# Diagonal of a 2-D prefix sum: row sums split by rows instead of columns, and the last 16 rows loaded early

## The chip, the cores and the metric

The kernel runs on one core of a Trainium2 chip. The metric is the device time of one execution in microseconds (us). Three runs of the kernel before took 667.54, 667.44 and 667.08 us; the median is 667.44.

## What is computed

```python
def setup_inputs():
    B, H, W = 4, 4224, 4224
    return {"x": np.random.randn(B, H, W).astype(np.float32)}

def reference(x):
    B, H, W = x.shape
    ps = np.cumsum(np.cumsum(x, axis=1), axis=2)
    N = min(H, W)
    diag = np.diagonal(ps, axis1=1, axis2=2)
    return np.cumsum(diag, axis=1).astype(np.float32)
```

Element i of an image's diagonal is the sum of the square x[0..i, 0..i]. It grows from i-1 to i by the part of row i left of and on the diagonal and the part of column i above it. So the kernel needs, for each i, one row sum up to the diagonal and one column sum down to it, and then two running sums over i. Every element of the four images is read once: 285 MB in float32.

## The kernel before, in words

**Staging.** An image has 11 groups of 384 rows and columns (GW = 384, NG = 11). The main loop takes strips of 768 rows: a strip is a tile `strip` of 128 partitions x 6 rows x 4224 columns in bf16, loaded by one DMA from GpSimd (POOL) that casts from float32 on the way (`load_rows`, L76). Images 0 to 2 take five such strips and one of 384 rows; the last image (LB = 3) takes four strips, two half strips, and then a finely cut end. There are three strip buffers (NBUF = 3), so the load of a strip waits until the strip three places earlier has been used up; POOL stands at that wait in program order. Nothing plans the order: instructions run on each engine as the program lists them.

**One strip** (`add_up`, L349). TensorE (PE) adds the columns right of the diagonal block with matmuls by a one-hot matrix (L226, L219). VectorE (DVE) multiplies the diagonal block by a mask (`mu`, L362) and subtracts (L363), so that the block keeps only the part left of the diagonal; where the next group's columns are summed by rows (`rowed`, L268), DVE does it next. Row sums then go up to column `hi`, the end of the diagonal block. They are split **by columns**: ScalarE (ACT) sums columns 0 to `ws` of each of the six rows (`act_sum`, L263, writing its unneeded copy to a tile `dump`), with ws = 9/16 of the block's first column, and DVE sums columns `ws` to `hi` of all six rows in one instruction (`acc`, L268). The two halves are added later (`sum_up`, L387).

**The end of the last image.** Its last 256 + 128 rows come in pieces: rows of `part_a` in two DMAs (L451), and the last 128 rows in five (L462). These five split 32 rows at a time into four pieces of 1024 columns each, so that 32 rows fill 128 partitions: blocks 0, 1, 2 whole, block 3 as columns 0 to 768 and 768 to 1024 of each quarter. POOL can have eight of these DMAs under way; the last two L462 issues wait for earlier landings. DVE (`pair_sum`, L277) and ACT (L263) add up what landed, PE weighs the sums into three small PSUM rows (`fin_a`, `fin_b`, `fin_e`, L219), and SyncE (SP) stores the results (L558 to L581). The very last chain is: landing of the last piece, `pair_sum`, three matmuls into `fin_e`, a copy (L580) and a store (L581).

**Other traffic.** `head`, the last 528 columns of 256 rows, is loaded first by SP's queue without a cast (L69) and used up at the start. Four images' results leave by SP: 11 rows of 3 x 384 at L558 (about 525 us), 10 rows of 384 at L561, and three single rows.

Of the kernel before, what the change touches and what calls it, by code (L numbers as in the profile page):

```python
# [17 lines left out]
def kernel(  # L18
# [30 lines left out]
    consts = ctx.enter_context(tc.tile_pool(name="consts", bufs=1))  # L49
    strips = ctx.enter_context(tc.tile_pool(name="strips", bufs=NBUF))  # L50
    mup = ctx.enter_context(tc.tile_pool(name="mup", bufs=1))
    dumpool = ctx.enter_context(tc.tile_pool(name="dump", bufs=1))
    smalls = ctx.enter_context(tc.tile_pool(name="smalls", bufs=2))
    last = ctx.enter_context(tc.tile_pool(name="last", bufs=1))
    psum_d = ctx.enter_context(
# [156 lines left out]
    weights4 = consts.tile([P, P], FP32, name="weights4")  # L212
    nc.vector.tensor_scalar_max(out=weights4, in0=steps, scalar1=0.0)

    ident_h = consts.tile([P, P], BF16, name="ident_h")
    nc.vector.tensor_copy(out=ident_h, in_=ident)

    def matmul(o, lhsT, rhs, start=False):
        nc.tensor.matmul(  # L219
            o, lhsT=lhsT, rhs=rhs, start=start, stop=False, skip_group_check=True  # L220
        )
# [36 lines left out]
    def act_sum(acc, src, own=None):  # L258
        w = src.shape[-1]
        dump = own  # L260
        if dump is None:
            dump = dumpool.tile([P, 2176], BF16, name="dump")
        nc.scalar.activation(  # L263
            out=dump[:, :w], in_=src, func=ACT.Copy, accum_out=acc
        )

    def row_sums(acc, src):
        nc.vector.reduce_sum(out=acc, in_=src, axis=AX.X)  # L268
# [26 lines left out]
            accum_out=acc,  # L295
        )

    def scalar_cols(r0):

        return r0 * 9 // 16 // 32 * 32  # L300
# [15 lines left out]
    for h in range(2):  # L316
        w = GW - h * P
        masked(hmu[:, h, :w], head[:, h, HC - w : HC], um1[:, :w], hu[:, h : h + 1])
    nc.vector.tensor_sub(out=asum[:, :, 0], in0=hs[:, 0:2], in1=hu[:, 0:2])

    whole_sums = last.tile([NG, LB, GW], FP32, name="whole_sums")
    last_sums = last.tile([NG, GW], FP32, name="last_sums")

    for b in range(B):
# [10 lines left out]
        def row_of(j):  # L335
            return (j + t0) % NG
# [9 lines left out]
            matmul(d[:, lo:hi], lhsT, rhs, start=first[0])  # L346
            first[0] = False

        def add_up(strip, f, r0, acc, um, wp=0, ws=None, by_rows=False):  # L349
# [8 lines left out]
            if ws is None:  # L358
                ws = scalar_cols(r0)
            mu = mup.tile([P, f, f * P], BF16, name=f"mu{f}")  # L360
            block = strip[:, :, r0:hi]
            nc.vector.tensor_mul(out=mu, in0=block, in1=um)  # L362
            nc.vector.tensor_sub(out=block, in0=block, in1=mu)  # L363
            if by_rows:
                rowed = mup.tile([P, GW], FP32, name="rowed")
                row_sums(
                    rowed,
                    strip[:, :, hi : hi + GW].rearrange("p q c -> p c q"),
                )
            for h in range(nw):  # L370
                for q in range(f):
                    columns(g + h, 0, GW, mu[:, q, h * GW : (h + 1) * GW], q > 0)
            if by_rows:
                k = row_of(g + nw)
                matmul(d, sel_f[:, NG - 1 - k : 2 * NG - 1 - k], rowed)
            for q in range(f):
                if ws > wp:
                    act_sum(acc[:, q, 0:1], strip[:, q, wp:ws])
            row_sums(acc[:, :, 1], strip[:, :, ws:hi])

        acc6 = smalls.tile([P, NS, F2, 2], FP32, name="acc6")
        acc3 = smalls.tile([P, 2, F, 2], FP32, name="acc3")
        nc.vector.memset(acc6[:, 0, :, 0], 0.0)

        def sum_up(acc):

            nc.vector.tensor_add(  # L387
                out=acc[..., 1], in0=acc[..., 1], in1=acc[..., 0]
            )

        ns = NS if whole else NS - 1
        for s in range(ns):
            strip = prefetched.pop(0) if prefetched else None
            if strip is None:
                strip = strip_tile()
                load_rows(strip, b, s * F2 * P)
            add_up(
                strip, F2, s * F2 * P, acc6[:, s], um6, by_rows=whole and s > 0
            )
            if not whole and s == 0:  # L400
                diag_b = last.tile([P, P], BF16, name="diag_b")
                nc.gpsimd.dma_start(out=diag_b, in_=x[b, TB:N, TB:N])
            if not whole and s == 1:
                row_sums(hs[:, 2:3], diag_b)
                masked(hmu[:, 2, :P], diag_b, um1[:, :P], hu[:, 2:3])
                nc.vector.tensor_sub(out=dtot, in0=hs[:, 2:3], in1=hu[:, 2:3])
                for h in range(3):
                    columns(LG, h * P, GW, hmu[:, h, : GW - h * P], h > 0)
        a6 = acc6[:, :ns]
        sum_up(a6)  # L410
        for h in range(2):
            ps = slice(h * HP, (h + 1) * HP)
            k = row_of(h)
            nc.vector.tensor_copy(  # L414
                out=r6[ps, k : k + 2 * ns : 2, :], in_=a6[ps, :, :, 1]
            )

        strip = strip_tile()
        if whole:
            load_rows(strip[:, :F], b, T0)  # L420
            add_up(strip[:, :F], F, T0, acc3[:, 0], um3)
            sum_up(acc3[:, 0])
            nc.vector.tensor_copy(out=r3[:, LG, :], in_=acc3[:, 0, :, 1])  # L423
        else:


            for h in range(2):
                load_rows(strip[:, h * F : h * F + F], b, T0 - (2 - h) * GW)
            add_up(strip[:, :F], F, T0 - 2 * GW, acc3[:, 0], um3)
            sum_up(acc3[:, 0])  # L430
            nc.vector.tensor_copy(out=r3[:, row_of(LG - 2), :], in_=acc3[:, 0, :, 1])
# [7 lines left out]
            add_up(strip[:, F:], F, T0 - GW, parts, um3, wp, ws)  # L439
            row_sums(parts[:, :, 2], fold_g)  # L440
            row_sums(r3[:, row_of(LG - 1), :], parts)

        if not whole:

            strip = strip_tile()
            part_a = strip[:, 0:2]
            part_b = strip[:, 2, :TB].rearrange("p (s c) -> p s c", s=4)
            spare = strip[:, 3, :]
            acuts = [(1536, N - HC), (0, 1536)]
            for c0, c1 in acuts:  # L450
                nc.gpsimd.dma_start(out=part_a[:, :, c0:c1], in_=src_a[:, :, c0:c1])  # L451
            CB = TB // 4
            bcut = 768
            for sb, c0, c1 in (
                (0, 0, CB),
                (1, 0, CB),
                (2, 0, CB),
                (3, 0, bcut),
                (3, bcut, CB),
            ):  # L460
                r0 = TB + sb * R
                nc.gpsimd.dma_start(  # L462
                    out=part_b[:, sb, c0:c1],
                    in_=x[b, r0 : r0 + R, :TB].rearrange("r (k c) -> r k c", k=4)[
                        :, :, c0:c1
                    ],
                )
# [112 lines left out]
        nc.vector.tensor_copy(out=ye, in_=fin_e)  # L580
        nc.sync.dma_start(out=out[b, T0 + E0 : N].unsqueeze(0), in_=ye)  # L581

# [29 lines left out]
```

## Time and profile before

| what | value |
|---|---|
| median of three runs | 667.44 us (667.08 to 667.54) |
| span of the profiled execution, first to last instruction | 665.7 us |
| own time of the profiled execution | not given by the page; the median lies 1.74 us above its span |
| DVE / PE / ACT / POOL busy | 379.8 / 214.2 / 135.3 / 31.7 us |
| DMA from POOL (queue 0) | 7312 packets, 142.47 MB written, 99.9% of 16 engines' time |
| DMA from SP (queue 1) | 342 packets, 0.61 MB, 0.3% |
| HBM read | 285.47 MB, 429 GB/s over the span |

The core has 16 DMA engines, and the share says how much of their time packets took. Times of the trace are counted from the first instruction of the span. Besides instructions the trace holds every DMA packet (start, duration, bytes written, queue) and, for each DMA, the times at which its semaphore was raised by the DMA engines that carried it. The packets carry no engine number, but each engine works through the same list of strip packets, so a packet's start plus a fixed step gives the next packet of the same engine, and each engine can be followed through the whole span.

### The profile page before, as it was taken

To read this page: it belongs to the slowest core of one execution; us is meant where nothing else is said; L and a number is where in the kernel's file an instruction comes from. 1 tells how busy PE (TensorE), PEld (TensorE's weight loads), DVE (VectorE), ACT (ScalarE), POOL (GpSimd) and SP (SyncE) were. 2 spreads that over 40 slices of the span, in tenths; PEclk is the share of its full clock that TensorE was granted. 3 is DMA by queue.
4 is the path that set the end of the run, shared out by engine and by line. 5 is a ranking of instruction groups with operands and counts; after the bars stand their busy time and mean duration, and the time that the engine had idled before them with its cause. 6 is when DMAs were issued, how large, how long until landed. Compare 5 with 4: busy or idle time off the path is not lost.

```text
span 665.7 us, 2592 instructions
## 1 busy us (share of the span) xinstructions
PE 214.2 (32%) x998; PEld 98.5 (15%) x998; DVE 379.8 (57%) x176; ACT 135.3 (20%) x219; POOL 31.7 (5%) x60
## 2 busy tenths in 40 slices
PE   0070522302118143140311623403031253250468
PEld 0030211100003021010100311201000121120224
DVE  4160928476946173756793526466589443352766
ACT  0000121406300103040630020304063002030433
POOL 4200000000000000000000000000000000001000
PEclk9995856566558585765555958567555595765779
DMA  9999999999999999999999999999999999999998
GB/s 203 219 218 219 219 219 219 209 212 216 219 221 216 218 220 217 219 216 210 216 218 218 219 216 218 219 218 219 216 212 216 221 218 215 218 218 219 215 206 163
DMA packets 7667, 143.25 MB, mean 215 GB/s; under 512 B 698, under 2 KB 998, under 8 KB 2150
## 3 DMA queue, kind: packets, MB, share of 16 engines
q0 software_dynamic: 7312, 142.47, 99.9%
q1 hardware_dynamic: 342, 0.61, 0.3%
q8 instruction: 8, 0.13, 0.1%
q14 instruction: 5, 0.04, 0.0%
HBM read 285.47 MB, written 0.07 MB: 429 GB/s over the span
## 4 chain that ended last, share of the span: by engine, by line
DVE 51%; another core or an unknown queue 35%; DMA 12%; PE 1%; issue 1%; POOL 1%; DVEq 0%; POOLq 0%
DVE acc L268 27%; DMA strip<-in_x_dram 12%; DVE mu L362 7%; DVE strip L363 7%; DVE rowed L268 7%; PE d L219 1%; DVE c L497 0%; DVE whole_sums L497 0%; POOL strip L462 0%; DVE pu L268 0%; DVE whole_sums L288 0%; POOL strip L451 0%; DVE acc L387 0%; DVE rows L414 0%
## 5 line engine op out<-in xcount | busy, mean ns | idle before, releaser
L263 ACT ACTIVATE dump<-strip 128x416 bf16<-128x416 bf16 (+5 forms) x105 | 122.0, 1161 | 519.4 <-DMA strip<-in_x_dram 516.7
L362 DVE TENSOR_TENSOR mu<-strip,um 128x4608 bf16<-128x4608 bf16 (+1 forms) x24 | 52.4, 2183 | 256.9 <-DMA strip<-in_x_dram 256.7
L268 DVE TENSOR_REDUCE acc<-strip 128x6 f32<-128x4608 bf16 (+6 forms) x23 | 195.9, 8518 | 0.4
L226 PEld LDWEIGHTS <-sel 128*11 128x11 bf16 x643 | 66.7, 104 | 474.8 <-issue 445.4
L219 PE MATMUL d<-strip,sel 128*11 128x384 bf16 x90 | 37.3, 415 | 279.9 <-DMA strip<-in_x_dram 279.9
L226 PE MATMUL d<-strip,sel 128*11 128x384 bf16 x441 | 117.1, 409 | 13.8 <-DMA strip<-in_x_dram 13.8
L363 DVE TENSOR_TENSOR strip<-strip,mu 128x4608 bf16<-128x4608 bf16 (+1 forms) x24 | 52.4, 2183 | 1.0
L219 PE MATMUL d<-mu,sel 128*11 128x384 bf16 x43 | 16.0, 373 | 108.4 <-DVE mu L362 108.4
L268 DVE TENSOR_REDUCE rowed<-strip 128x384 f32<-128x2304 bf16 x12 | 48.9, 4076 | 0.0
L226 PE MATMUL d<-mu,sel 128*11 128x384 bf16 x200 | 45.7, 363 | 0.0
L76 POOL DMA_DIRECT2D strip<-in_x_dram x23 | 15.7, 683 | 537.2 <-DVE acc L268 291.8
L263 ACT ACTIVATION_READ_ACCUMULATOR dump<-strip 128x1 f32 x105 | 19.5, 186 | 0.0
L219 PE MATMUL d<-rowed,sel_f 128*11 128x384 f32 x24 | 11.7, 573 | 21.7 <-DVE rowed L268 21.7
L219 PEld LDWEIGHTS <-sel 128*11 128x11 bf16 x134 | 13.7, 102 | 24.8 <-issue 12.7
L219 PE MATMUL d<-ident,rows 128*11 128x128 f32 x24 | 5.2, 378 | 16.8 <-DVE rows L423 16.8
L219 PE MATMUL fold<-um,ident_h 128*128 128x512 bf16 x28 | 7.9, 454 | 0.0
L268 DVE TENSOR_REDUCE pu<-d 11x1 f32<-11x384 f32 x4 | 2.2, 546 | 6.2 <-PE d L219 6.2
L102 DVE MEMSET um<- 128x4608 bf16 (+1 forms) x2 | 4.9, 2458 | 1.1 <-issue 1.1
L103 POOL TENSOR_SCALAR_AFFINE_SELECT um<-um 128x4608 bf16<-128x4608 bf16 (+1 forms) x2 | 5.2, 2612 | 7.2 <-DVE um L102 7.2
L219 PEld LDWEIGHTS d<-rowed,sel_f 128*11 128x11 f32 x24 | 1.4, 92 | 26.4 <-DVE rowed L268 26.1
L219 PEld LDWEIGHTS d<-ident,rows 128*11 128x11 f32 x24 | 2.6, 118 | 18.5 <-DVE rows L423 11.7
L219 PE MATMUL d<-halves,rows 128*11 128x64 f32 x48 | 5.3, 289 | 0.0
(119 smaller groups left out, 75.0 us busy)
## 6 DMA issues: line engine op xcount, KB each, us to landing
strip<-in_x_dram POOLq DMA_DIRECT2D x18, 6336.0 KB, 72.7
strip<-in_x_dram POOLq DMA_DIRECT2D x7, 3168.0 KB, 55.7
strip<-in_x_dram POOLq DMA_DIRECT2D x1, 1080.0 KB, 49.9
strip<-in_x_dram POOLq DMA_DIRECT2D x1, 768.0 KB, 52.9
strip<-in_x_dram POOLq DMA_DIRECT2D x3, 256.0 KB, 54.1
head<-in_x_dram SPq DMA_DIRECT2D x1, 528.0 KB, 3.9
strip<-in_x_dram POOLq DMA_DIRECT2D x1, 192.0 KB, 43.2
strip<-in_x_dram POOLq DMA_DIRECT2D x1, 64.0 KB, 28.6
```

What stands on the lines that cost most here:

```text
L76: nc.gpsimd.dma_start(out=o, in_=x[b, r0 : r0 + f * P, :].rearrange("(p f) w -> p f w", f=f))
L102: nc.vector.memset(um, 1.0)
L103: nc.gpsimd.affine_select(out=um, in_=um, compare_op=ALU.is_gt, fill=0.0, base=0, pattern=[[-1, f], [1, f * P]], channel_multiplier=-f,)
L219: nc.tensor.matmul(o, lhsT=lhsT, rhs=rhs, start=start, stop=False, skip_group_check=True)
L226: te.add_instruction(mybir.InstMatmult(start_tensor_calc=False, stop_tensor_calc=False, tile_position=(0, 0), tile_size=(P, P if lhsT.shap ...
L263: nc.scalar.activation(out=dump[:, :w], in_=src, func=ACT.Copy, accum_out=acc)
L268: nc.vector.reduce_sum(out=acc, in_=src, axis=AX.X)
L362: nc.vector.tensor_mul(out=mu, in0=block, in1=um)
L363: nc.vector.tensor_sub(out=block, in0=block, in1=mu)
```

## The change

Three edits.

1. **Row sums split by rows.** In the main loop ACT now sums three whole rows of the six (columns 0 to `hi`), one instruction each, and DVE the other three in one instruction; in the 384-row strips ACT sums two rows and DVE one. ACT writes its copy back over the row it reads, and `dump` is gone. ACT therefore starts a strip after the subtraction (L363) instead of at the strip's landing. Both write straight into one sum tile, so `sum_up` goes. The last half strip of the last image keeps its old split.
2. **The last 16 rows load early.** Columns 0 to 4095 of the last 16 rows (E = 16) of the last image are loaded in float32 into the used-up tile `head`, as 64 pieces of 4 KB, by DMAs that ACT issues after the third strip of image 0. For three of the four column quarters they go as two DMAs of 8 rows, for the fourth as one DMA of 16: seven DMAs. DVE sums them in image 3 (`end_sums`), and one more matmul weighs them into `fin_e`.
3. **The last block has 16 rows.** Block 3 of the end, formerly 32 rows in four quarters, now holds the 16 rows that are left, in eight pieces of 512 columns each, again over 128 partitions and in two DMAs of 256 columns. ACT's share of its first half shrinks from 320 to 128 columns and DVE's from 448 to 128; the last DMA is 256 columns on 128 partitions as before. New weight tiles for both are built at the start.

```diff
-    dumpool = ctx.enter_context(tc.tile_pool(name="dump", bufs=1))
...
+    E = P // 8
+    steps8 = consts.tile([P, R], I32, name="steps8")
+    nc.gpsimd.iota(steps8, pattern=[[8, R]], base=15, channel_multiplier=-1)
...
+    weights8 = consts.tile([P, R], FP32, name="weights8")
+    nc.vector.tensor_scalar_max(out=weights8, in0=steps8, scalar1=0.0)
...
+    weights_e = consts.tile([P, E], FP32, name="weights_e")
+    nc.vector.tensor_scalar_max(out=weights_e, in0=place, scalar1=0.0)
...
         if dump is None:
-            dump = dumpool.tile([P, 2176], BF16, name="dump")
+            dump = src
...
+    CB = TB // 4
+    ends = head.rearrange("p h c -> p (h c)")[: 4 * E, :CB]
+    end_sums = last.tile([4 * E, 1], FP32, name="end_sums")
...
-            for q in range(f):
-                if ws > wp:
+            if fs:
+                for q in range(fs):
+                    act_sum(acc[:, q : q + 1], strip[:, q, :hi])
+                row_sums(acc[:, fs:], strip[:, fs:, :hi])
+            else:
+                for q in range(f):
                     act_sum(acc[:, q, 0:1], strip[:, q, wp:ws])
-            row_sums(acc[:, :, 1], strip[:, :, ws:hi])
...
+                row_sums(acc[:, :, 1], strip[:, :, ws:hi])
...
+            if b == 0 and s == 2:
+
+                for k in range(4):
+                    n = E // 2 if k < 3 else E
+                    for r in range(0, E, n):
+                        nc.scalar.dma_start(
+                            out=ends[k * E + r : k * E + r + n],
+                            in_=x[
+                                LB,
+                                N - E + r : N - E + r + n,
+                                k * CB : (k + 1) * CB,
+                            ],
+                        )
...
             if not whole and s == 1:
+                row_sums(end_sums, ends)
...
-            bcut = 768
-            for sb, c0, c1 in (
-                (0, 0, CB),
-                (1, 0, CB),
-                (2, 0, CB),
-                (3, 0, bcut),
-                (3, bcut, CB),
+            CE = TB // 8
+            bcut = CE // 2
+            for sb, rows, c0, c1 in (
+                (0, R, 0, CB),
+                (1, R, 0, CB),
+                (2, R, 0, CB),
+                (3, E, 0, bcut),
+                (3, E, bcut, CE),
             ):
...
+        matmul(fin_e[:, R - E :], end_sums, weights_e[: 4 * E])
...
-        act_sum(esum[:, 0:1], part_b[:, 3, :320], spare[:, 960:1280])
-        pair_sum(esum[:, 1:2], part_b[:, 3, 320:bcut])
-        pair_sum(esum[:, 2:3], part_b[:, 3, bcut:])
+        act_sum(esum[:, 0:1], part_b[:, 3, : bcut // 2], spare[:, 960 : 960 + bcut // 2])
+        pair_sum(esum[:, 1:2], part_b[:, 3, bcut // 2 : bcut])
+        pair_sum(esum[:, 2:3], part_b[:, 3, bcut:CE])
...
-            matmul(fin_e, esum[:, k : k + 1], weights4[:, :R])
+            matmul(fin_e, esum[:, k : k + 1], weights8)
```

More of the change, by code (lines that the diff above doesn't have):

```diff
@@ L213 @@
     nc.vector.tensor_scalar_max(out=weights4, in0=steps, scalar1=0.0)
+    E = P // 8
+    steps8 = consts.tile([P, R], I32, name="steps8")
+    nc.gpsimd.iota(steps8, pattern=[[8, R]], base=15, channel_multiplier=-1)
+    nc.vector.tensor_single_scalar(
+        out=steps8, in_=steps8, scalar=3, op=ALU.arith_shift_right
+    )
+    weights8 = consts.tile([P, R], FP32, name="weights8")
+    nc.vector.tensor_scalar_max(out=weights8, in0=steps8, scalar1=0.0)
+    row_in = consts.tile([P, E], I32, name="row_in")
+    nc.gpsimd.iota(row_in, pattern=[[0, E]], base=0, channel_multiplier=1)
+    nc.vector.tensor_single_scalar(
+        out=row_in, in_=row_in, scalar=E - 1, op=ALU.bitwise_and
+    )
+    place = consts.tile([P, E], I32, name="place")
+    nc.gpsimd.iota(place, pattern=[[1, E]], base=1, channel_multiplier=0)
+    nc.vector.tensor_sub(out=place, in0=place, in1=row_in)
+    weights_e = consts.tile([P, E], FP32, name="weights_e")
+    nc.vector.tensor_scalar_max(out=weights_e, in0=place, scalar1=0.0)
     ident_h = consts.tile([P, P], BF16, name="ident_h")
@@ L296, in masked @@
         )
-    def scalar_cols(r0):
-        return r0 * 9 // 16 // 32 * 32
     rows6, rows3 = [], []
@@ L347, in columns, with add_up @@
             first[0] = False
-        def add_up(strip, f, r0, acc, um, wp=0, ws=None, by_rows=False):
+        def add_up(strip, f, r0, acc, um, fs=0, wp=0, ws=0, by_rows=False):
             nw = f * P // GW
@@ L357, in add_up @@
                     columns(j, 0, GW, strip[:, q, j * GW : (j + 1) * GW], q > 0)
-            if ws is None:
-                ws = scalar_cols(r0)
             mu = mup.tile([P, f, f * P], BF16, name=f"mu{f}")
@@ L375, in add_up @@
                 matmul(d, sel_f[:, NG - 1 - k : 2 * NG - 1 - k], rowed)
-            for q in range(f):
-                if ws > wp:
-                    act_sum(acc[:, q, 0:1], strip[:, q, wp:ws])
-            row_sums(acc[:, :, 1], strip[:, :, ws:hi])
[L381 to L389, printed above, removed]
+            if fs:
[4 more added lines that the diff above has]
+                for q in range(f):
+                    act_sum(acc[:, q, 0:1], strip[:, q, wp:ws])
+                row_sums(acc[:, :, 1], strip[:, :, ws:hi])
+        acc6 = smalls.tile([P, NS, F2], FP32, name="acc6")
         ns = NS if whole else NS - 1
@@ L397 @@
             add_up(
-                strip, F2, s * F2 * P, acc6[:, s], um6, by_rows=whole and s > 0
+                strip, F2, s * F2 * P, acc6[:, s], um6, F, by_rows=whole and s > 0
             )
+            if b == 0 and s == 2:
[9 more added lines that the diff above has]
+                            ],
+                        )
             if not whole and s == 0:
@@ L409 @@
         a6 = acc6[:, :ns]
-        sum_up(a6)
         for h in range(2):
@@ L414 @@
             nc.vector.tensor_copy(
-                out=r6[ps, k : k + 2 * ns : 2, :], in_=a6[ps, :, :, 1]
+                out=r6[ps, k : k + 2 * ns : 2, :], in_=a6[ps]
             )
@@ L420 @@
             load_rows(strip[:, :F], b, T0)
-            add_up(strip[:, :F], F, T0, acc3[:, 0], um3)
-            sum_up(acc3[:, 0])
-            nc.vector.tensor_copy(out=r3[:, LG, :], in_=acc3[:, 0, :, 1])
+            add_up(strip[:, :F], F, T0, r3[:, LG], um3, F - 1)
         else:
@@ L428 @@
                 load_rows(strip[:, h * F : h * F + F], b, T0 - (2 - h) * GW)
-            add_up(strip[:, :F], F, T0 - 2 * GW, acc3[:, 0], um3)
-            sum_up(acc3[:, 0])
-            nc.vector.tensor_copy(out=r3[:, row_of(LG - 2), :], in_=acc3[:, 0, :, 1])
+            add_up(strip[:, :F], F, T0 - 2 * GW, r3[:, row_of(LG - 2)], um3, F - 1)
             ready = psum_s.tile([P, 512], FP32, name="fold")
@@ L438 @@
             parts = last.tile([P, F, 3], FP32, name="parts")
-            add_up(strip[:, F:], F, T0 - GW, parts, um3, wp, ws)
+            add_up(strip[:, F:], F, T0 - GW, parts, um3, wp=wp, ws=ws)
             row_sums(parts[:, :, 2], fold_g)
@@ L451 @@
                 nc.gpsimd.dma_start(out=part_a[:, :, c0:c1], in_=src_a[:, :, c0:c1])
-            CB = TB // 4
-            bcut = 768
-            for sb, c0, c1 in (
-                (0, 0, CB),
-                (1, 0, CB),
-                (2, 0, CB),
-                (3, 0, bcut),
-                (3, bcut, CB),
+            CE = TB // 8
[6 more added lines that the diff above has]
+                (3, E, bcut, CE),
             ):
@@ L463 @@
                     out=part_b[:, sb, c0:c1],
-                    in_=x[b, r0 : r0 + R, :TB].rearrange("r (k c) -> r k c", k=4)[
-                        :, :, c0:c1
-                    ],
+                    in_=x[b, r0 : r0 + rows, :TB].rearrange(
+                        "r (k c) -> r k c", k=P // rows
+                    )[:, :, c0:c1],
                 )
```

## The prediction

> **What bounds the kernel now.** I read the page's queue part first, then the waits, then the end of the chain and its timeline.
>
> ```profile
> span 665.7 us, 2592 instructions
> PE 214.2 (32%) x998; PEld 98.5 (15%) x998; DVE 379.8 (57%) x176; ACT 135.3 (20%) x219; POOL 31.7 (5%) x60
> ...
> DMA  9999999999999999999999999999999999999998
> ...
> q0 software_dynamic: 7312, 142.47, 99.9%
> q1 hardware_dynamic: 342, 0.61, 0.3%
> ```
>
> POOL's queue fills the 16 DMA engines for 99.9% of the span, and no compute engine is busy for more than 57%. The loads are the bound. In the packet records every engine starts one 25,344-byte strip piece (50,688 bytes read) every 1.867 us, throughout. The waits and the issues say that this queue is never short of work:
>
> ```profile
> POOL strip L76 <- DVE acc L268: 291.8, 9, 34.8
> ...
> POOL strip L462 <- DMA strip<-in_x_dram: 26.4, 2, 14.4
> ```
>
> ```profile
> strip<-in_x_dram POOLq DMA_DIRECT2D x18, 6336.0 KB, 72.7
> ```
>
> POOL does wait for buffers, but a strip lands 72.7 us after its issue, while 16 pieces of 1.867 us need only 29.9 us: more than a strip is always queued ahead of a new one. The end of the chain, from 640 us on, and the instructions in it:
>
> ```profile
> 619.41 43.19 DMA strip<-in_x_dram
> 662.60 0.03 issue
> 662.62 0.41 DVE pair L277 x2
> 663.03 0.04 issue
> 663.08 0.47 PE fin_e L219 x6
> 663.55 0.02 issue
> 663.57 0.18 DVE ye L580
> ```
>
> ```profile
> 662.62 0.39 DVE L277 SCALAR_TENSOR_TENSOR pair<-strip 128x224 f32<-128x224 bf16 x1
> ...
> 662.96 0.29 DVE L277 SCALAR_TENSOR_TENSOR pair<-strip 128x128 f32<-128x128 bf16 x1
> ...
> 663.78 0.23 SPq L581 DMA_DIRECT2D out_dram<-ye  x1
> ```
>
> After the last landing (662.93 in the semaphore records) come one pair sum, matmuls, a copy and a store. So the time is set by **the last of the 16 DMA engines to finish**, plus a fixed 2.8 us to the span's end. The engines don't finish together. The last DMA's 16 semaphore steps run from 661.35 to 662.93, 1.58 us apart. Followed back, the engines' lags behind the first at 640 us are 0, 0.11, 0.14, 0.19, 0.29, 0.29, 0.73, 0.83, 1.08, 1.09, 1.09, 1.24, 1.30, 1.32, 1.36, 1.59 us; the 0.73 engine falls to 1.23 after an instruction fetch at 657.65. The lags come from instruction fetches (queue 8, 16 KB each, at 71, 195, 264, 373, 458, 563 and 638 us): each sets one engine back by 1.1 us, each time another one. The 1.59 engine lost 0.75 us in the first 7 us and 0.32 to an 8 KB fetch at 354.6.
>
> **The row split.** DVE's sums of 4608 and 12672 elements took 4.95 and 13.35 us, that is 1.04 ns an element and 0.16 fixed. Three rows up to `hi` are 2304 to 11520 elements in place of 4608 to 12672: 2.56 against 4.95 in a first strip, 12.15 against 13.35 in a fifth. Over all strips DVE loses some 44 us of sums and 1.4 of `sum_up` (8 x 0.17), and gains 1.2 for `end_sums` (nearest row: `hs`, 1056 columns, 1.25). ACT took 0.550 us for 416 and 1.990 for 2144 columns: 0.833 ns each plus 0.20, and 0.19 for the accumulator. A fifth strip costs it 3 x 3.59 = 10.8 us. It now starts behind L363, 5.2 us after the landing: done 16.0 us after it, where DVE ends at 5.2 + 4.0 (`rowed`) + 12.15 = 21.4 (22.6 before). In a first strip ACT ends last, at 8.3 against DVE's 10.1 before. Behind ACT's longer wait stands only its own next strip, 29.9 us away. Buffers come free 1 to 2 us earlier and POOL issues earlier into a full queue: worth **0 us** on the path. The cover is that queue, 72.7 - 29.9 = 43 us deep; were it gone, a strip would pay that 21.4 us chain. In the last image DVE stood until 635.87 on a strip that followed at 634.11; it gains 1.6 there, but its next input lands at 649.02, so nothing ends earlier.
>
> **Setup.** Three iotas and five small DVE operations of 0.1 to 0.25 us (rows `steps`, `hu`) fall before the first strip lands at 35.4, behind the POOL issues of the first loads: 0.
>
> **The seven DMAs of ACT.** SP's issues take 0.23 to 0.44 us each; seven cost ACT 1.6 to 3.1 us about 110 us in, and it then has some 15 us without work: 0. They wait for `head`'s load alone, landed at 4.67. SP's later stores wait for semaphores long raised; POOL's instruction and semaphore order is unchanged. What they cost is engine time. A piece of 4096 bytes read and written isn't in the trace. From the strip pieces (50,688 bytes read in 1.867 us) it is 0.151 us; from `head` (2112 bytes every 0.082) 0.159; from the 11-row store, whose eleven engines each lost 0.195 us to three pieces of 1536 bytes, 0.173. I take 0.152, since strip pieces are also limited by the float32 side, and 0.005 for the semaphore packet.
>
> How many engines does a DMA of 8 rows use? The 11-row store raised its semaphore in 12 steps, the 10-row store in 11, a single row in 2: one step at once and then one per row. So 8 rows go to 8 engines, one piece each. The packets show more: the ten engines of the second store are all among the eleven of the first. The Trainium skill, "DMA: Bandwidth & Descriptors", section "Why a DMA increments its semaphore by 16 and not by 1", says that such a DMA takes the lowest-numbered engines; by that rule the eight are always the same and lie among those ten, which the trace's two stores bear out. So I take eight of the ten. They get 6 + 1 = 7 pieces, 7 x 0.157 = **+1.10 us**; the other eight get one, +0.16.
>
> **The smaller last block.** Per engine, 8 pieces of 1536 bytes at 0.1166 us and 8 of 512 at 0.041 become 16 of 512 at 0.041: 1.26 less 0.66 is **-0.60 us** on all sixteen. Net: eight engines +0.50, eight -0.44.
>
> **Which engines?** The last engine (662.626) carried a piece of the 10-row store, at 662.630, right behind its own last packet: it is one of the ten, and so are those at 1.36, 1.32 and 1.23. Only two of ten escape. If the last one is among the eight (8 in 10), the last landing moves by **+0.50**. If it escapes, the engine at 1.36 or 1.32 is among the eight and ends at 1.36 + 0.50 = 1.86 against 1.59: +0.27 (or +0.23).
>
> **The end chain.** The last DMA has the same shape, so pair sum, matmuls, copy and store stay. ACT's 320 columns and DVE's 448 get smaller, off the path. One matmul more at about 660.3, of 0.22 us like its `fin_e` neighbours, delays PE's chain, which has 0.38 us of idle time before 663.08: 0.
>
> **Sum.** 0 + 0 + 1.10 - 0.60 = +0.50. Span 665.7 to 666.2; the runs' median lies 1.74 above the span, hence 667.44 + 0.50 = **667.9 us**. By pieces of 0.151 to 0.173 the sum is +0.49 to +0.64.
>
> **The rivals.**
>
> *The last engine escapes*: +0.25, 667.7. For: two places in ten; also the 0.32 us fetch at 354.6 may fall elsewhere, since ACT has some 90 instructions fewer. Against: eight in ten.
>
> *The change doesn't do what it says, and the pieces spread over all sixteen*: 4 each, 4 x 0.157 - 0.60 = +0.03, 667.5. Against it stand the 12 and 11 semaphore steps.
>
> *The late engines escape, and the end comes earlier*: -0.44, 667.0. It needs all the late engines outside the eight, as if the ones carrying extra were the early five (0 to 0.29). For: five of the ten are early, and five of the six others late (1.08 to 1.30). Against: the four latest among the ten don't fit in two places; only lags that fall otherwise in other runs would do it.
>
> *The eight neighbouring partitions choke* (this ends slower). All eight pieces of a DMA are written to eight neighbouring partitions, which no load of the trace does. Longest for such pieces are `head`'s first ones, 0.34 to 0.93 us for 2112 bytes. At 0.6 us each, six pieces cost 6 x (0.60 - 0.15) = 2.7 more: +3.2, 670.6. It decides from 0.29 us a piece, where the +0.50 grows past 1.33. Against: the 11-row store read eleven neighbouring partitions at 0.065 us a piece, near full rate, and the engines' lags spread the pieces over 1.6 us. The Trainium skill, "SBUF — State Buffer", section "Door 1: The DMA port swizzle", speaks for it: four neighbouring partitions share a port of about 27 GB/s, so eight rows of 4 KB on two ports would need an estimated 0.6 us; by that rule the sum would be near +3 us, and no run here shows a load of that shape.
>
> **How the numbers follow.** A measurement of this kernel can tell about 0.2%, 1.33 us, from no change; "same" is 666.1 to 668.8. Chances: forecast 0.55; last engine escapes 0.13; spread over sixteen 0.10; late engines escape 0.08; choke 0.10; something faster by over 0.2% that I don't see 0.04. That gives faster 0.04, same 0.86, slower 0.10. The range takes in all but the last two, with the runs' own 0.2 us scatter and some partial choking above: 666.8 to 668.9.
>
> **What would show it.** Right: the last DMA's semaphore steps split wider, some 2.4 us from first (0.14 - 0.44) to last (1.59 + 0.50), eight engines each 1 us further behind the rest after 110 us, 1.867 us elsewhere; DVE near 336 us busy, ACT near 166; POOL's queue still at 99.9%; the last landing near 663.4. Wrong: 4 KB pieces over 0.3 us, gaps in POOL's queue, or a last landing below 662.6.

## The result, and the profile after

The kernel after takes **668.18 us** (median of 21 runs, 667.9 to 669.7) where the kernel before took 667.42 in the same session (21 runs, 667.03 to 669.12). The ratio is 1.0014, with a 95% interval of 1.0008 to 1.0019: slower by some 0.5 to 1.3 us, less than the 1.33 us that the prediction calls a measurable difference. The forecast was 667.9, +0.5. The profiled execution took 669.7 us with a span of 668.0, the longest of its 21 runs (median span 666.5), so its absolute times lie about 1.5 us late; differences inside it are what the readings below use.

The head of the page, its queue part and its DMA issues:

```profile
span 668.0 us, 2549 instructions
PE 213.4 (32%) x999; PEld 98.1 (15%) x1000; DVE 335.9 (50%) x166; ACT 154.2 (23%) x145; POOL 32.0 (5%) x63
...
q0 software_dynamic: 7312, 142.34, 99.5%
q1 hardware_dynamic: 342, 0.61, 0.4%
q10 hardware_dynamic: 128, 0.26, 0.1%
...
strip<-in_x_dram POOLq DMA_DIRECT2D x18, 6336.0 KB, 73.5
...
head<-in_x_dram ACTq DMA_DIRECT2D x6, 32.0 KB
```

The kernel is still bound by POOL's queue. DVE lost 44 us of work, and the strips still land 73.5 us after their issue (72.7 before). ACT's queue is new: q10, of whose 128 packets 64 are the 4 KB pieces.

The end is another story. The chain of work that ended last, from 640 us on:

```profile
639.49 7.28 PE fold L238 x27
646.77 4.25 another core or an unknown queue
651.07 0.58 PE fold L238
651.65 4.31 PE fold L245 x11
...
660.41 0.16 DVE carry L515
...
660.59 1.01 DVE c L517
...
661.62 1.02 DVE last_sums L517
...
662.68 0.32 PE fin_b L238 x2
663.00 0.19 PE fin_e L238 x4
...
665.23 0.25 PE fin_e L238 x8
...
665.50 0.18 DVE ye L601
```

Before, this chain went back to the landing of a late `part_b` DMA. Now it goes back to the landing of the last **half strip** at 651.02, and from there through TensorE and DVE to the final copy without a wait for a DMA: 14.5 us of work. The timelines of VectorE and TensorE say the same:

```profile
663.67 0.46 DVE L296 SCALAR_TENSOR_TENSOR pair<-strip 128x288 f32<-128x288 bf16 x1
...
664.31 0.41 DVE L578 TENSOR_TENSOR yl<-fin_a,last_sums 1x256 f32<-1x256 f32 x1 [0.17 <-PE fin_a L238]
664.65 0.20 DVE L296 SCALAR_TENSOR_TENSOR pair<-strip 128x64 f32<-128x64 bf16 x1
...
664.79 0.27 DVE L296 SCALAR_TENSOR_TENSOR pair<-strip 128x128 f32<-128x128 bf16 x1
...
665.50 0.18 DVE L601 COPY ye<-fin_e 1x32 f32<-1x32 f32 x1 [0.43 <-PE fin_e L238]
```

```profile
665.13 0.34 PE L238 MATMUL fin_e<-weights,esum 128*1 128x32 f32 x6
```

The last semaphore step is at 664.33, but DVE first finishes the sums of earlier blocks and begins the last pair sum at 664.79. TensorE's last six matmuls stood behind 0.38 us of idle time in the kernel before:

```profile
663.08 0.45 PE L219 MATMUL fin_e<-weights,esum 128*1 128x32 f32 x6 [0.38 <-DVE pair L277]
```

Now they have none. From the last landing to the copy it is 1.17 us, 0.64 before.

The end of a kernel can be put on one scale: last semaphore step of the last load, start of the final copy (`ye`), end of the span. The landing is from the semaphore records, the other two from timeline and page, one profiled execution each:

```
kernel           landing   copy after   span ends     landing to
                 (us)      landing      after copy    span's end
before           662.93    0.64         2.13          2.77
after            664.33    1.17         2.48          3.65
```

So of the 2.3 us that lie between the two profiled spans, 0.88 arose behind the last landing, in the part that the prediction took for fixed.

### The profile page after: what moved, and what is told of

It reads as the page before. It is cut to its first block, busy times and chain, and to the rows that moved or that the text cites. A ratio compares the mean times of both kernels' runs of the same rounds, so it can differ in the third digit from the quotient of the medians.

```text
span 668.0 us, 2549 instructions
## 1 busy us (share of the span) xinstructions
PE 213.4 (32%) x999; PEld 98.1 (15%) x1000; DVE 335.9 (50%) x166; ACT 154.2 (23%) x145; POOL 32.0 (5%) x63
## 3 DMA queue, kind: packets, MB, share of 16 engines
q0 software_dynamic: 7312, 142.34, 99.5%
## 4 chain that ended last, share of the span: by engine, by line
another core or an unknown queue 43%; DVE 37%; PE 10%; DMA 5%; ACT 3%; issue 1%; POOL 0%; DVEq 0%; ACTq 0%; POOLq 0%
DVE acc L287 16%; DVE rowed L287 7%; DVE mu L377 6%; DVE strip L378 6%; PE d L245 5%; DMA strip<-in_x_dram 5%; ACT strip L282 3%; PE d L238 2%; PE fold L238 1%; PE fold L245 1%; DVE c L517 0%; DVE whole_sums L517 0%; DVE pu L287 0%; DVE whole_sums L307 0%
## 5 line engine op out<-in xcount | busy, mean ns | idle before, releaser
L282 ACT ACTIVATE strip<-strip 128x768 bf16<-128x768 bf16 (+9 forms) x71 | 150.2, 2115 | 482.4 <-DVE strip L378 475.6
L287 DVE TENSOR_REDUCE acc<-strip 128x3 f32<-128x2304 bf16 (+4 forms) x19 | 134.8, 7092 | 0.2
L238 PE MATMUL d<-strip,sel 128*11 128x384 bf16 x90 | 37.0, 411 | 288.5 <-DMA strip<-in_x_dram 288.5
L245 PE MATMUL d<-strip,sel 128*11 128x384 bf16 x441 | 115.6, 406 | 13.8 <-DMA strip<-in_x_dram 13.8
L287 DVE TENSOR_REDUCE rows<-strip 128x1 f32<-128x4224 bf16 (+1 forms) x4 | 17.4, 4353 | 0.1
L282 ACT ACTIVATION_READ_ACCUMULATOR strip<-strip 128x1 f32 x71 | 13.2, 186 | 0.0
## 6 DMA issues: line engine op xcount, KB each, us to landing
strip<-in_x_dram POOLq DMA_DIRECT2D x18, 6336.0 KB, 73.5
```

The lines of the kernel that those rows point to most:

```text
L238: nc.tensor.matmul(o, lhsT=lhsT, rhs=rhs, start=start, stop=False, skip_group_check=True)
L245: te.add_instruction(mybir.InstMatmult(start_tensor_calc=False, stop_tensor_calc=False, tile_position=(0, 0), tile_size=(P, P if lhsT.shap ...
L282: nc.scalar.activation(out=dump[:, :w], in_=src, func=ACT.Copy, accum_out=acc)
```

## The experiments

Two theories stood against each other. **L**: the last engine of the 16 sets the end, so each packet added or removed on it counts in full. **C**: the chain of compute behind the last half strip has become as long as the landings, so the smaller last block (-0.60 us of packets per engine) gains little or nothing. All experiments were run beside the kernel before, in three sessions, in which it took 667.43 us (`extra8` to `all16`), 667.72 (`split` and the *short* kernels) and 667.64 (the *onescan* kernels and `after_warm`). First all results in one table; "time" is the median minus that of the kernel before in the same session, "span" the same difference of the median spans. The ratio is worked out from all runs and isn't always the quotient of the two medians.

```
kernel           time us (runs)   against before    ratio, 95%               span
extra8           668.91 (7)       +1.48             1.0025 (1.0014-1.0035)   +1.5
extra8x2         670.03 (5)       +2.60             1.0040 (1.0028-1.0052)   +2.5
small            667.50 (12)      +0.07             1.0005 (0.9997-1.0014)   -0.25
all16            668.77 (10)      +1.34             1.0019 (1.0011-1.0028)   +1.2
split            667.78 (12)      +0.06             1.0003 (0.9993-1.0013)   -0.3
before_short     667.77 (11)      +0.05             1.0001 (0.9993-1.0010)   -0.1
after_short      668.98 (11)      +1.26             1.0017 (1.0008-1.0025)   +0.6
small_short      667.83 (11)      +0.11             1.0002 (0.9993-1.0011)   -0.5
before_onescan   667.48 (11)      -0.16             1.0000 (0.9991-1.0009)   -0.1
small_onescan    667.68 (11)      +0.04             1.0001 (0.9991-1.0010)   -0.4
after_onescan    668.62 (11)      +0.98             1.0017 (1.0009-1.0026)   +1.0
after_warm       668.26 (11)      +0.62             1.0012 (1.0003-1.0021)   +0.6
```

### The early DMAs alone, once and twice

The kernel before, with the seven DMAs added and their data unused (`extra8`); the same with fourteen (`extra8x2`: `s in (2, 3)`, the second seven into other partitions).

```diff
+            if b == 0 and s == 2:
+                for k in range(4):
+                    n = E // 2 if k < 3 else E
+                    for r in range(0, E, n):
+                        nc.scalar.dma_start(
+                            out=ends[k * E + r : k * E + r + n],
...
```

> The kernel before, with the seven early DMAs added and nothing else (their data isn't used; the row split, the last block and the sums stay as before). In the changed kernel's trace each 4 KB piece held its engine 0.168 us, so eight engines lose 7 x 0.168 = 1.18 us and eight 0.17. Both theories: every later landing on those eight moves by 1.18, so the time rises by 1.0 to 1.2 us if the last engine is one of the eight, and by about 0.9 (1.18 less the 0.27 by which the last engine led the next) if it is not. If the early load is not what costs: within 0.2 us of before.

> The kernel before with fourteen early DMAs, the seven of the change twice, after strips 3 and 4 of image 0 (data not used). Eight engines lose 2.36 us. If the last engine is one of the eight: twice the rise of the single set, 2.2 to 2.4 us. If it escapes: 2.1, and more than twice the single set's 0.9. If a piece costs by something else than its engine's time (issue on ScalarE, one-off stall): well under twice.

Measured +1.48 and +2.60 us. L and C say the same here; both times grow as they say, and both lie a little above. The packet records of the kernel after give the size of a piece: 64 packets of 4096 bytes, each 0.172 us long, seven on each of eight engines and one on each of the other eight. Each sets its engine back by 0.168 us against its strip pieces, so seven cost 7 x 0.168 = 1.18 and fourteen 2.36. In `extra8` three of the 64 lasted longer, 0.19 to 0.31 us; none came near the 0.6 us of the choking rival. The last landings moved to 664.08 and 665.08, 1.15 and 2.15 later than in the kernel before's profile.

What is left, 0.2 to 0.3 us, lies behind the landing. In both, the end of the chain is the old one (`extra8`):

```profile
620.56 43.18 DMA strip<-in_x_dram
...
663.76 0.41 DVE pair L277 x2
...
664.22 0.47 PE fin_e L219 x6
...
664.71 0.18 DVE ye L597
```

The copy is again 0.63 us after the landing, but the span ends 2.33 us after the copy, where it was 2.13. The instruction records of SP show why. At the end of a program SP waits for a row of semaphores, one wait every 0.06 us. In the kernel before, the wait for the last store's own semaphore ($S[116]) is the last of the row, at 664.82, and the closing instruction follows at 664.89. In `extra8` that store's semaphore is $S[115]; it is through at 665.98, and three more waits follow before the closing instruction at 666.23. With the seven DMAs the row is longer, and more of it stands behind the last store: **+0.2 us**, whatever the loads do. In `extra8x2` four more waits follow, and the span ends 2.38 us after the copy.

### The smaller last block without the early DMAs, and the row split alone

`small` is the kernel after without the seven DMAs, `end_sums` and its matmul; it leaves columns 0 to 4095 of the last 16 rows out of the result. `split` is the kernel before with the row split only.

```diff
-            if b == 0 and s == 2:
-                for k in range(4):
...
-                row_sums(end_sums, ends)
...
-        matmul(fin_e[:, R - E :], end_sums, weights_e[: 4 * E])
```

> The changed kernel without the early DMAs and without end_sums: row split and 16-row last block stay, columns 0 to 4095 of the last 16 rows are left out of the result. Theory L (the prediction's: the end follows the last landing): 0.60 us less on every engine, time -0.6 us. Theory C (the compute chain from the landing of the last half strip to the last store, 14.5 us in both profiles, is as late as the last landing, with 0.1 to 0.4 us to spare before): -0.1 to -0.4 us, the rest of the 0.6 is lost.

> The kernel before with the row split alone (first edit; no early load, last block of 32 rows). Both theories: 0, within 0.2 us of before, with VectorE some 45 us less busy. A gain or loss here would mean that the split touches the path.

`split` took +0.06 us and `small` +0.07: the row split is worth nothing, as forecast, and the smaller last block, alone with it, gains **nothing** that the run times show, where L expected -0.6 and C -0.1 to -0.4 (the median span does lie 0.25 lower). The packets did get cheaper. In the profiles of the three kernels with the small block and no early DMA the last landing is at 662.19, 662.55 and 661.98 us; in the three forms of the kernel before it is at 662.93, 662.94 and 662.69: 0.61 earlier in the mean. The end doesn't follow. VectorE in `small`:

```profile
661.51 0.46 DVE L296 SCALAR_TENSOR_TENSOR pair<-strip 128x288 f32<-128x288 bf16 x1 [0.57 <-DMA strip<-in_x_dram]
...
661.90 0.41 DVE L563 TENSOR_TENSOR yl<-fin_a,last_sums 1x256 f32<-1x256 f32 x1
662.23 0.20 DVE L296 SCALAR_TENSOR_TENSOR pair<-strip 128x64 f32<-128x64 bf16 x1
...
662.37 0.27 DVE L296 SCALAR_TENSOR_TENSOR pair<-strip 128x128 f32<-128x128 bf16 x1
...
662.97 0.18 DVE L586 COPY ye<-fin_e 1x32 f32<-1x32 f32 x1 [0.31 <-PE fin_e L238]
```

From block 2's pair sum (288 columns), which here waits 0.57 us for its own landing, to the copy DVE has 1.46 us of its own work and of TensorE's, and no wait for a DMA in it. The kernel before had 1.87 us there:

```profile
661.70 0.46 DVE L277 SCALAR_TENSOR_TENSOR pair<-strip 128x288 f32<-128x288 bf16 x1 [0.76 <-DMA strip<-in_x_dram]
...
663.57 0.18 DVE L580 COPY ye<-fin_e 1x32 f32<-1x32 f32 x1 [0.31 <-PE fin_e L219]
```

Its two pair sums of block 3, at 662.62 and 662.96, began right behind their landings at 662.60 and 662.93. Landings of block 3 that come earlier can be used only until block 2's landing and the 1.46 us behind it are the limit. The copy is 0.78 us after the landing in `small`, 1.01 in `small_short` and 1.21 in `small_onescan`, against 0.64 before, so 0.14 to 0.57 of the 0.60 is lost on the way.

Where the rest went isn't shown. The run time of `small`, `split`, `small_short` and `small_onescan` lies 2.06 to 2.08 us above the span in the median, that of the kernel before 1.72 to 1.74, that of the kernel after 1.70. These 0.33 us cancel the 0.25 to 0.5 by which the four spans are shorter. But `split` has both (span -0.3) with the old block, so they come with the row split and not with the smaller block; why was not found. Against `split`, the smaller block shortens the median span by 0.2 us at the most (-0.25, -0.5 and -0.4 against -0.3), which these runs can hardly tell from nothing.

### Sixteen rows per early DMA

`all16` is the kernel after with four early DMAs of 16 rows, so that every engine gets four pieces.

```diff
-                    n = E // 2 if k < 3 else E
+                    n = E
```

> The changed kernel with all four early quarters as DMAs of 16 rows, so that every one of the sixteen engines gets 4 pieces in place of 7 and 1. 4 x 0.168 = +0.67 us on every engine, -0.60 in the last block. Theory L: +0.07 us against before, 0.5 less than the changed kernel. Theory C: the half strip lands 0.67 later and the chain behind it keeps its length, so +0.3 to +0.6.

Measured +1.34 us, far above L and above C's range too. Its last landing is at 663.02, +0.09 against the kernel before, where L works out 4 x 0.168 - 0.60 = +0.07. L is right on the landing, and the landing doesn't set the end: DVE begins the last pair sum 0.47 us after it.

```profile
663.49 0.27 DVE L296 SCALAR_TENSOR_TENSOR pair<-strip 128x128 f32<-128x128 bf16 x1
```

From the landing to the copy it is 1.18 us, 0.54 more than before: that part is C's. Behind the copy come 2.64 us, 0.51 more than before: the last store is issued 0.14 later behind the copy, and six closing waits of SP follow its semaphore's ($S[112], through at 665.59; the closing instruction follows at 666.03). About 0.2 more lies outside the span (median 1.94 us, 1.73 for the kernel before) and isn't explained. The last half strip's mask starts at 649.81 us, 649.12 before: it lands 0.7 us later, since the engines have carried the four pieces by then but gain from the smaller block only behind it; and the chain behind it was already almost as long as the landings. The same holds for the kernel after: between the landing of the half strip and that of the last block are 13.91 us before and 13.31 after, exactly the 0.60 less. The chain from the half strip's landing to the copy takes 14.48 us in the kernel after; it was 14.55 before, with 0.38 us of waiting for the landing in it.

### Taking work out of the chain behind the half strip

Three edits, each in one or more of the kernels. *short*: the fold of 1920 columns by 12 matmuls becomes one of 160, so 1760 columns of the last group's row sums are left out.

```diff
-            fold_in(fold_g, strip[:, F:], 0, wp, 160, start=True)
+            fold_in(fold_g, strip[:, F:], 0, 160, 160, start=True)
```

> The kernel before with the compute chain behind the last half strip cut: 11 of the 12 fold matmuls are left out (1760 of the 1920 columns that TensorE folds are missing from the row sums of the last group), about 3.7 us of TensorE in that chain. Theory L: 0, the last landing decides. Theory C: 0 to -0.2, since before both ends are nearly equal; the pair sum of the last DMA starts at its landing and the chain's slack is there.

> The changed kernel with the same cut of 11 fold matmuls (same columns left out). Theory L: as the changed kernel, +0.5 to +0.8 against before. Theory C: the last landing decides again and the 0.60 of the smaller block counts, so 0.3 to 0.5 us below the changed kernel, +0.2 to +0.6 against before; the last pair sum starts at its landing.

> The kernel 'small' (no early DMAs, 16-row last block, last 16 rows left out) with the same cut of 11 fold matmuls. Theory L: as 'small', -0.6. Theory C: -0.6 here, where 'small' without the cut gives only -0.1 to -0.4.

*onescan*: the last image is summed once instead of twice, one 1.02 us DVE instruction less.

```diff
-        for i, (to, src) in enumerate(((c1, d), (c2, c1))):
+        for i, (to, src) in enumerate(((c1, d), (c2, c1)) if whole else ((c2, d),)):
```

> The kernel before with one of the two running sums of the last image left out (the second scan reads d directly; the last image's result lacks one summation). That takes 1.04 us out of the chain from the last half strip's landing to the last copy and changes nothing else. Theory L and theory C agree: the last landing decides here, time 0 to -0.1 us, last landing to copy 0.64 us as before.

> The kernel 'small' (16-row last block, no early DMAs, last 16 rows left out) with the same scan left out. 'small' measured +0.0 to +0.1 us where 0.60 less was due, and its copy came 0.78 us after the last landing in place of 0.64. Theory C: with 1.04 us out of the chain the landing decides, copy 0.64 us after it, time 0.3 to 0.6 us below before. Theory L: as 'small'. If the 0.60 isn't there in the landings at all (the engines' lags take it): as 'small' too, but with the copy at 0.64.

> The changed kernel with the same scan left out. The changed kernel's copy came 1.17 us after its last landing. Theory C: 0.64 here, time 0.4 to 0.5 us below the changed kernel, +0.2 to +0.5 against before. Theory L: no difference from the changed kernel (+0.76).

*warm*: 40 instead of 28 idle matmuls ahead of the half strip, with the full result.

```diff
-            for i in range(28):
+            for i in range(40):
```

> The changed kernel with 40 in place of 28 matmuls that keep TensorE busy before the last half strip lands. In the changed kernel TensorE stood idle 4.25 us ahead of that strip (2.80 before), and its fold of that strip took 4.9 us at a granted clock of 0.50 (4.0 at 0.74 before). Theory C with the clock as its cause: idle time about 1 us, fold under 4.1 us at a clock of 0.7 or more, copy 0.64 to 0.8 us after the last landing, time 0.3 to 0.5 us below the changed kernel. If the clock isn't the cause: copy still 1.1 us after the landing and +0.76.

In run time no edit of a kernel with the small block brought what C expected. `before_short` (+0.05) and `before_onescan` (-0.16) stay at the kernel before, as both theories say. `small_short` and `small_onescan` stay at +0.11 and +0.04; `after_short` and `after_onescan` aren't below the kernel after at all, and `after_warm` is at +0.62 where the kernel after is at +0.76, within what these runs can tell.

The profiles say more. Their lengths, one execution each: TensorE's idle time ahead of the last half strip, the granted clock in the 4 us from its landing, and from that landing the start of the carry copy (DVE, `carry`, right behind TensorE's sums) and of the final copy:

```
kernel           idle   clock   carry   final copy
before           2.8    0.61    8.56    14.55
split            4.6    0.61    8.73    14.48
extra8           3.7    0.66    8.72    14.54
extra8x2         2.2    0.61    8.73    14.52
before_onescan   3.6    1.00    7.69    14.60
before_short     3.6    0.69    9.37    14.52
small            4.5    0.62    8.73    14.10
after_onescan    4.8    0.57    8.78    14.09
after_warm       2.9    1.00    7.69    14.08
after_short      4.5    0.62    9.05    14.15
after            4.3    0.50    9.38    14.48
all16            4.3    0.50    9.38    14.48
small_onescan    5.5    0.50    9.79    14.52
small_short      5.6    0.50    9.60    14.70
```

With the old block (the first six) the last landing decides, and the copy comes 14.5 to 14.6 us behind the half strip whatever the clock. With the small block it comes at 14.08 to 14.15 where the clock was 0.57 or more, and at 14.48 to 14.70 where it was 0.50. So it is at the low clock that the chain is the limit, as far as one execution of each shows. That also accounts for the misses: in `small_onescan` the carry came 1.06 us later than in `small`, which ate the 1.02 us instruction that was left out, and the shorter fold of the *short* kernels didn't bring the carry forward, except by 0.33 us in `after_short`.

The chain isn't the only floor. In `after_onescan` and `after_warm` a landing is waited for again (DVE waits 0.84 and 0.81 us for block 2's), yet the copy comes 0.80 and 0.79 us behind the last landing, not 0.64: DVE's 1.46 us from block 2 on remain. The chain costs the kernel after at most the 0.38 us between 1.17 and 0.79. `after_warm` came to the clock, fold and copy that its expectation names for C (idle time 2.9 us where 1 was expected), but its run time doesn't show the 0.3 to 0.5 us.

Does the row split lower the clock? With it VectorE reaches the mask of the half strip before last 0.6 us after that strip's landing in the kernel after, 2.4 before; the 28 idle matmuls start 3.4 us after it, 4.2 before; and TensorE stands idle for longer before the last half strip lands (4.3 to 5.6 us with the split and 28 idle matmuls, 2.2 to 3.7 without the split). But the length of the idle time doesn't order the clocks: `split` and `small` had 0.61 and 0.62 after 4.6 and 4.5 us, the kernel before 0.61 after 2.8. The stretches of 4 us from the landing on, whose last three columns are granted clock, DMA share and GB/s, in the kernel before, the kernel after and `after_warm`:

```profile
649.00:653.00 4.00, 3.93 (x12) 1.46 (x12) 3.77 (x3) 3.83 (x6) 0.00 (x0) 0.61 1.06 215
```

```profile
651.00:655.00 4.00, 3.93 (x10) 1.50 (x11) 3.77 (x3) 3.79 (x6) 0.00 (x0) 0.50 1.06 213
```

```profile
650.00:654.00 4.00, 3.97 (x27) 2.10 (x28) 3.85 (x4) 3.79 (x6) 0.00 (x0) 1.00 1.04 209
```

In these 4 us TensorE begins 10 matmuls at a clock of 0.50 in the kernel after, 12 at 0.61 before and 27 at full clock with 40 idle matmuls. The traces' clock records show why such means differ: the granted clock is 1 or 0.5 and changes only in steps of 3.413 us, and these steps lie differently against the landing in each execution. Half clock lasted from 648.67 to 652.09 before (landing at 649.02), from 652.08 to 655.49 in `split` (landing at 651.21) and from 648.92 to 655.75, two steps, in the kernel after (landing at 651.02). So the 0.50 of the kernel after may be the lot of one execution. A longer idle time leaves more room for a second step at half clock, but that the split causes it isn't shown.

### The account

The lengths behind the last landing, one profiled execution of each:

```
kernel           landing   copy after   span ends     landing to
                 (us)      landing      after copy    span's end
before           662.93    0.64         2.13          2.77
before_short     662.94    0.64         2.19          2.83
before_onescan   662.69    0.63         2.13          2.77
split            665.05    0.64         2.13          2.77
extra8           664.08    0.63         2.33          2.96
extra8x2         665.08    0.64         2.38          3.02
small            662.19    0.78         2.14          2.92
after_warm       663.28    0.79         2.33          3.12
after_onescan    663.71    0.80         2.33          3.13
after_short      663.63    0.85         2.47          3.32
small_short      662.55    1.01         2.25          3.27
after            664.33    1.17         2.48          3.65
all16            663.02    1.18         2.64          3.82
small_onescan    661.98    1.21         2.25          3.46
```

In all six kernels with the old block the copy comes 0.63 or 0.64 us behind the last landing, in all eight with the small block 0.78 to 1.21. (`split` shows how far one execution can lie from another: one engine was 2.5 us behind at the first strip's landing and 2.3 behind the next one at the end.) For the kernel after: pieces +1.18 on eight engines, smaller block -0.60, copy later behind the landing +0.15 to +0.53, SP's closing waits +0.2, and SP's last store 0.13 later behind the copy where the store ahead of it was late. That is +0.9 to +1.4 where the last engine is one of the eight, and a few tenths less where it escapes; measured +0.76. The runs don't settle how often it escapes, nor why the run times of `extra8` and the kernel after differ by 0.7 us where these terms give 0 to 0.5.

## Why the prediction was right, and where not

The size and the direction came out: +0.76 us measured, +0.50 forecast, both within 0.2% of the kernel before, and 668.18 lies in the range. By its steps:

- **What bounds the kernel**: right. The queue is still at 99.5%, `extra8` and `extra8x2` add per piece what the pieces cost, and no experiment that only relieved an engine made the kernel quicker.
- **The row split, 0**: right on the time (`split` +0.06). DVE came to 335.9 us (336 forecast). ACT came to 154.2, not 166: a row took what was forecast (3.39 us for 3840 columns), but the forecast added up instructions, and the 0.19 us in which an accumulator is read lies under the next row's sum: the rows of one strip start 2.12 us apart, with 2.11 us each. Missed were a longer idle time of TensorE ahead of the last half strip (4.3 us, 2.8 before; that it lowered the clock isn't shown), and the 0.33 us outside the span in the kernels with the split and no early DMAs.
- **Setup and ACT's issues, 0**: right for the issues. Six of the seven took 2.28 us on ACT's queue at 101 us, beside its own work. Missed was what more DMA semaphores cost at the very end: +0.2 us.
- **The seven DMAs, +1.10 on eight engines**: the mechanism was right, the term was undersized. Eight engines got seven pieces each and the others one, as worked out from the steps of the stores. A piece took 0.168 us of its engine, not 0.157, inside the forecast's own bounds (0.151 to 0.173): +1.18.
- **The eight neighbouring partitions choke**: didn't happen, every piece took 0.172 us in the kernel after. The eight pieces of a DMA weren't under way at once: from the start of the first to the end of the last it was 0.80 us in the kernel after, as long as the engines' lags spread them. The prediction's estimate of 0.6 us for eight such rows, from the Trainium skill, "SBUF — State Buffer", section "Door 1: The DMA port swizzle", is shorter than that, so this load doesn't test it.
- **The smaller last block, -0.60**: right for the packets, wrong for the time. With the pieces the forecast had the last landing near 663.4; it is at 664.33 in the long profiled execution, and at 663.63, 663.71 and 663.28 in `after_short`, `after_onescan` and `after_warm`, 0.69 later in the mean of these three than in the mean of the three forms of the kernel before, where +0.50 was forecast.
- **The end chain, 0**: this is the step that failed. "The last DMA has the same shape, so pair sum, matmuls, copy and store stay" is true of the instructions and not of their start. The prediction took the path for "last landing plus a fixed 2.8 us"; that stretch measured 3.65 in the kernel after, and 3.12 and 3.13 in `after_warm` and `after_onescan`, where the end waits for landings. Two things were there to be read before: 13.91 + 0.64 = 14.55 us from the half strip's landing to the copy, of which TensorE, whose work fills nearly all of it, stood idle for 0.38 at the end; and DVE's order, in which block 2's pair sum, an addition and two more pair sums stand ahead of the copy. The 0.38 us of TensorE's idle time before its last matmuls was read as cover for one matmul; it was the slack of the whole end, and close to what earlier landings were worth here (0.45 at the most, 0.60 less the 0.15 by which the copy came later behind the landing).
- **Which engines**: left open by the runs, as told above. The last DMA's steps came 2.61 us apart (2.39 to 2.77 in `after_warm`, `after_short` and `after_onescan`), where about 2.4 was forecast.

That the time came near the forecast is partly luck. A gain of 0.60 was counted in full that gave 0.45 at the most, and costs of 0.3 to 0.4 were left out; by the terms of the account the time should lie further above. What made up for it, perhaps that the last engine isn't one of the eight in every execution, isn't shown.

## What to carry to other kernels

Where one queue is full from start to end, moving bytes to an earlier place in it bought nothing here: the early pieces cost 1.18 us on their engines and took 0.60 off the end, and no variant here beat the kernel before. Before an earlier landing is counted as a gain, measure the next-longest chain to the same end, here the one from the half strip, and take the smaller of the two slacks as the limit. A DMA of 8 rows loads 8 of the 16 engines, so seven small DMAs can be dearer than their bytes (262 KB are 0.67 us spread over sixteen engines and 1.18 us on eight), though here the even spread of `all16` was no better, since the half strip waited all the same.

## What the runs showed of the hardware that was not expected

- A 4096-byte piece on a second queue beside a full stream lasted 0.172 us in 64 of 64 packets of the kernel after and set its engine back by 0.168 (0.180 in eight of the 64).
- The granted clock of TensorE is 1 or 0.5 and changes only at steps of 3.413 us. Over the 14 traces here, TensorE's work in one step told the clock of the next: a step at full clock was followed by half clock in all cases with a busy share of its matmul records under 0.41 and in none over 0.46 (712 steps), and a step at half clock by full clock in none under 0.71 and in all over 0.77 (1852 steps). So 2.2 us of idle time can be enough, as in `extra8x2`, where it fell into one step, and 3.6 us can be too little, as in `before_onescan`, where they fell half into one step and half into the next.
- The engine count of such a DMA was exact: 8 rows on eight engines, always the same eight over six DMAs. That agrees with the Trainium skill, "DMA: Bandwidth & Descriptors", section "Why a DMA increments its semaphore by 16 and not by 1", by which such a DMA takes the lowest-numbered engines; the records bear no numbers, so only the sameness is seen here.
- More DMAs lengthen the end of the program: closing waits of 0.06 us each came to stand behind the last store's, three (0.2 us) in the kernel after, its three variants `after_short`, `after_onescan` and `after_warm`, and `extra8`, four in `extra8x2` and six in `all16`, where the store's semaphore stands earlier in the row.
- The 16 engines don't start together. The steps of the first strip's DMA lay 0.22 us apart in `after_warm` and 2.47 in `split`, and in `split` the last engine was still 2.3 us behind the next at the end. Such starts may well be what spreads the runs of one kernel by a microsecond or two (667.03 to 669.12 for the kernel before); that wasn't tested.
- Run time and span don't differ by a constant: in the median 1.70 to 1.84 us in the others, 1.94 in `all16`, 2.06 to 2.08 in the four with the row split and no early DMAs. A change of a few tenths has to be judged by the run time, and this case's span gains of 0.25 to 0.5 us vanished in it.
